# An encoder layer in one kernel: wider maxima, transposed spreads, split weights kept in DRAM, and attention exponentials handled two key tiles at a time

## The chip, the cores and the metric

The kernel runs as one program on one core of a Trainium2 chip (trn2). The metric is device time in microseconds for one execution; lower is better. Before the change three timed runs gave 3049.92, 3058.68 and 3075.47 us, with a median of 3058.68 us. One further execution was taken with the hardware profiler; all rows shown here come from it.

In the rows PE is the matrix engine, PEld its loading of the stationary operand, DVE the vector engine, ACT the scalar engine, POOL the third elementwise engine, and SP the engine whose queue issues nearly all the DMAs. L149 is line 149 of the kernel file. Every engine works through its own list of instructions strictly in the order in which it was written out; between engines there are only semaphores.

## What is computed

One layer of an encoder on a sequence of 2048 tokens of width 1024, all in float32. Cut to what matters:

```python
h = x @ w_in                                    # 2048 x 1024 -> q, k, v of A; low-rank q, kv of B; u, v of C
y_a = dilated attention, 6 heads of 64, patterns (128,1), (512,4), (2048,16), ALiBi,
      each a band of 64 keys to either side at its dilation, merged by log-sum-exp
c_q = rms(h[...]) * q_norm;  q = c_q @ w_q_up   # 6 heads, 64 plain + 32 rotary columns
c_kv = rms(h[...]) * kv_norm; kv = c_kv @ w_kv_up
y_b = softmax(q_full @ k_full.T * 96**-0.5) @ v # 6 heads, all 2048 keys
y_c = u * (w_s @ layer_norm(v) + b_s)           # in chunks of 128 tokens, 4 groups
y = concat(rms(y_a), rms(y_b), rms(y_c)) * mix_norm
x = layer_norm(ALPHA * x + y @ w_out)
f = square(relu(x @ w_ff1 + b_ff1)) @ w_ff2 + b_ff2
out = layer_norm(ALPHA * x + f)
```

The result has to agree with float32. The kernel gets there by splitting every operand into a rounded part (`h`, "high") and the rest (`l`, "low"), both in a reduced float32 type, and adding three matrix products: high by high, low by high and high by low. `mm3` (lines 148 to 151) is that triple; most of PE's time is spent in it.

## The kernel before

The program runs through five stages, whose borders can be read from the trace.

**First columns (about 0 to 225 us).** `latent_columns` takes the sequence in four blocks of 512 tokens. `load_x` fetches the eight 128-row pieces of x for a block, and ACT and DVE split each into high and low. Weights are fetched by `load_wf`, split likewise and kept. PE computes the low-rank columns (`psf`), the gating columns (`psg`) and, one block behind, the projections up to the heads' q, k and v (`psk`, `psq`, `psv`). Results go to scratch tensors in DRAM.

**Projection with latent attention (about 225 to 690 us), then dilated attention with latent attention (to about 1450 us), then the output projection with the rest of latent attention (to about 1700 us).** The function `mixers` interleaves two streams: latent attention (`latent`) always, and one filler after the other (`projection`, `dilated`, `out_projection`). Fixed rates (RATE_P, RATE_D, RATE_O) say how many filler steps follow a latent step; the Tile framework then places the instructions by its own estimate of when their operands are ready, and the result is one fixed list for each engine.

*Projection* fetches x again for blocks 0 to 2 (the last block's x is still there), splits it again, and for each block fetches the 768 columns of weights for q and k of A in twelve pieces and those of v in four (`load_w`, line 454), splitting each piece on ACT (L460) and DVE (L461). So every weight is split four times. Results are again stored in high and low parts in DRAM.

*Latent attention* works on 24 steps (6 heads by 4 blocks of 512 queries) of 16 key tiles each. For one key tile of 128 keys: three products give the scores `st` (L612 to L614); ACT takes the exponential twice, once in float32 (`pr`, L619) and once rounded (`ph`, L620); POOL subtracts them to the low part `pl` (L622); DVE adds `pr` to the running sum `ac` (L637; for key tile 8 POOL does it); and PE multiplies the values by `ph` and by `pl` into `av` (L644, L645). The maxima that are subtracted are found one or two steps ahead: 16 products `mx` (L593), each with a reduction on DVE (L594), and a last reduction `m4` whose four columns PE turns into a row (`mr`, L601). At the end of a step PE sums `ac` over the partitions with four products by a column of ones (`dn`, L665), DVE takes the reciprocal, and `spread` (L164) multiplies that column, repeated 64 times, by the identity, which puts it along the free axis of 64 partitions (`rb`). `spread` is also used with 128 partitions in the first stage and in the output projection.

*Dilated attention* has 20 groups of tiles in each of 6 heads. A first pass finds maxima: for each tile one product `amx` of 64 rows (queries by keys, high parts only, L866) and one fused DVE operation (L871). A second pass makes the scores with two products of 128 and 65 rows (L939, L940), the exponential, and the product with the values (L996). In SBUF the tile `QA` holds the high part of q twice (rows 0 to 63 and 64 to 127), and `KA` holds the high part of k above its low part.

**Feed-forward (about 1700 us to the end).** Two large products with a Strassen-like scheme of seven products each; nothing in it is touched.

## Time and profile before

| what | value |
|---|---|
| median of three runs | 3058.68 us (3049.92 to 3075.47) |
| the profiled execution's own time | 3056.2 us |
| its span, first to last instruction | 3054.4 us |
| PE busy | 2900.1 us, 95% of the span |
| PE weight loads busy | 2311.9 us, 76% |
| DVE busy | 2154.3 us, 71% |
| POOL busy | 1653.3 us, 54% |
| ACT busy | 1336.7 us, 44% |
| mean granted clock of PE | 0.962 of full |
| moved by DMA | 314.02 MB, mean 103 GB/s |

How to read it: busy time is the time in which an instruction of the engine was under way. Matrix products are pipelined, so one that is listed with 0.39 us may be followed by the next 0.23 us after its start; the distance between two starts is what a product costs PE. A busy PE is therefore not a PE at its peak. The granted clock is 1.00 when PE runs at 2.4 GHz and 0.50 when it runs at 1.2 GHz; other values are means over a stretch that has both.

### The profile page before, as it was taken

The page shows a single profiled execution, that of the slowest core. Times are in us where ns is not written, and L with a number is a line of the kernel's source. Part 1 is how long each engine was busy: PE and PEld are TensorE (multiplying, and loading weights), DVE is VectorE, ACT ScalarE, POOL GpSimd, SP SyncE. Part 2 cuts the span into 40 slices and gives each one's busy share as a digit, 9 for nine tenths or more (in the row PEclk, how much of TensorE's full clock was granted, in tenths as well). Part 3 has the DMA queues.
Part 4 walks back from the last instruction along what each step waited for, and adds up shares of the span by engine and source line. Part 5 has one row for each costly group of instructions (what it writes and reads, how often), then busy time and mean ns, then how long its engine had stood idle before and what let it go on. Part 6 is the DMA issues. An engine that isn't in the chain of part 4 may idle for free. (4 is left out here: it accounts for less than half of the span.)

```text
span 3054.4 us, 38546 instructions
## 1 busy us (share of the span) xinstructions
PE 2900.1 (95%) x12716; PEld 2311.9 (76%) x12716; DVE 2154.3 (71%) x3519; ACT 1336.7 (44%) x2504; POOL 1653.3 (54%) x1251
## 2 busy tenths in 40 slices
PE   9999899999999999998899999989999999999996
PEld 7776777887776777777787778867887877777774
DVE  4247889878877878788776843383335787778899
ACT  4325455556543544455554534353434322223333
POOL 1015556557644544456865454454445765656667
PEclk9999999999998999898999999999999999999998
DMA  5345334236022342213255533333334422222222
GB/s 165 125 136 162 107 106 128 79 116 128 14 59 47 76 88 48 54 41 89 90 174 181 162 122 111 108 115 119 106 108 166 138 80 83 83 77 76 83 66 97
DMA packets 267762, 314.02 MB, mean 103 GB/s; under 512 B 91805, under 2 KB 157981, under 8 KB 267037
## 3 DMA queue, kind: packets, MB, share of 16 engines
q1 hardware_dynamic: 254248, 295.82, 32.5%
q10 hardware_dynamic: 13312, 15.73, 1.4%
q8 instruction: 100, 1.64, 0.2%
q14 instruction: 102, 0.83, 0.1%
HBM read 209.72 MB, written 98.60 MB: 101 GB/s over the span
## 5 line engine op out<-in xcount | busy, mean ns | idle before, releaser
L622 POOL TENSOR_TENSOR pl<-pr,ph 128x512 fp32r<-128x512 f32 x384 | 553.3, 1453 | 410.8 <-ACT ph L620 271.8
L637 DVE TENSOR_TENSOR ac<-ac,pr 128x512 f32<-128x512 f32 x312 | 355.1, 1138 | 65.1 <-ACT pr L619 56.3
L1572 DVE TENSOR_TENSOR acc<-o,acc 128x512 f32<-128x512 f32 x416 | 275.2, 682 | 112.0 <-PE o L151 109.5
L619 ACT ACTIVATE pr<-st 128x512 f32<-128x512 f32 x384 | 227.9, 597 | 252.6 <-PE st L614 228.5
L594 DVE TENSOR_REDUCE m<-mx 128x1 f32<-128x512 f32 x384 | 254.9, 681 | 56.9 <-PE mx L593 56.0
L620 ACT ACTIVATE ph<-st 128x512 fp32r<-128x512 f32 x384 | 224.4, 596 | 43.9 <-PE av L644 39.2
L644 PE MATMUL av<-ph,VV 128*128 128x512 f32 x384 | 163.8, 426 | 14.1 <-DVE y L659 13.8
L645 PE MATMUL av<-pl,VV 128*128 128x512 f32 x384 | 167.9, 437 | 7.9 <-POOL pl L622 7.9
L612 PE MATMUL st<-QH,KL 96*128 96x512 f32 x384 | 167.6, 436 | 4.8 <-ACT ph L620 3.5
L593 PE MATMUL mx<-KH,QH 96*128 96x512 f32 x384 | 158.8, 435 | 12.2 <-DVE UV L424 4.6
L613 PE MATMUL st<-QL,KH 96*128 96x512 f32 x384 | 158.8, 414 | 0.0
L614 PE MATMUL st<-QH,KH 97*128 97x512 f32 x384 | 158.4, 415 | 0.0
L996 PE MATMUL aav<-apr,v 128*65 128x128 f32 (+3 forms) x624 | 123.8, 344 | 4.2 <-ACT apr L965 4.0
L1500 DVE TENSOR_TENSOR t<-t,h 128x512 f32<-128x512 f32 x32 | 21.9, 686 | 138.3 <-PE h L151 127.0
L871 DVE CUSTOM_DVE_ANT_0 jk<-amx,bias 128x256 bf16<-128x256 f32 (+2 forms) x288 | 103.2, 358 | 17.1 <-PE amx L866 9.9
L996 PEld LDWEIGHTS aav<-apr,v 128*65 128x65 f32 x624 | 85.6, 149 | 38.6 <-issue 9.3
L965 ACT ACTIVATE apr<-tt 128x192 f32<-128x192 f32 (+2 forms) x180 | 78.4, 467 | 82.9 <-PE aav L996 53.6
L939 PE MATMUL ast<-QA,KA 128*128 128x256 f32 (+1 forms) x288 | 105.7, 372 | 0.2 <-ACT ph L620 0.2
L149 PE MATMUL po<-woh,y 128*128 128x512 f32 x256 | 104.2, 407 | 0.0
L940 PE MATMUL ast<-QB,KB 65*128 65x256 f32 (+1 forms) x288 | 102.2, 368 | 1.5 <-DMA QB<-amr 1.0
L644 PEld LDWEIGHTS av<-ph,VV 128*128 128x128 f32 x384 | 79.1, 206 | 30.7 <-DVE y L659 16.9
L150 PE MATMUL po<-woh,y 128*128 128x512 f32 x256 | 101.5, 396 | 0.0
(9014 smaller groups left out, 8775.8 us busy)
## 6 DMA issues: line engine op xcount, KB each, us to landing
A<-in_w SPq DMA_DIRECT2D x128, 256.0 KB, 2.7
hid_d<-t SPq DMA_DIRECT2D x128, 256.0 KB, 3.0
A<-hid_d SPq DMA_DIRECT2D x128, 256.0 KB, 2.9
B<-in_w_ff SPq DMA_DIRECT2D x64, 256.0 KB, 4.2
xr<-in_xT SPq DMA_DIRECT2D x56, 256.0 KB, 3.3
wr<-in_wf SPq DMA_DIRECT2D x48, 256.0 KB, 3.3
yr<-y_d SPq DMA_DIRECT2D x64, 128.0 KB, 2.7
xt<-in_x SPq DMA_DIRECT2D x32, 256.0 KB, 3.4
```

Of the source, the lines that this page charges most:

```text
L593: pe.matmul(ps, s["QH"][0:96, qt * P:(qt + 1) * P], kh[0:96, kc * TB:(kc + 1) * TB], start=True, stop=True)
L594: dve.tensor_reduce(s["m16"][:, qt, kc:kc + 1], ps, AX.X, ALU.max)
L612: pe.matmul(st, kl[0:96, kk], s["QH"][0:96], start=True, stop=False)
L613: pe.matmul(st, kh[0:96, kk], s["QL"][0:96], start=False, stop=False)
L619: act.activation(pr, st, AF.Exp, scale=SC)
L620: act.activation(ph, st, AF.Exp, scale=SC)
L622: pool.tensor_tensor(pl, pr, f(ph), op=ALU.subtract)
L637: (pool if kt in AC_POOL else dve).tensor_tensor(s["ac"], s["pr"] if kt == 1 else s["ac"], pr, op=ALU.add)
L644: pe.matmul(s["av"], VV[h][:, kt], ph, start=(kt == 0), stop=False)
L645: pe.matmul(s["av"], VV[h][:, kt], pl, start=False, stop=(kt == NT - 1))
L996: pe.matmul(s[key][0:65, c0:c0 + w], s["V"][p][:, units[u][2] + j], pr[:, a0:a0 + w], start=(first[key] == i), stop=(last[key] == i), skip ...
L1572: dve.tensor_tensor(t, ps, t, op=ALU.add)
```

## The change

There are four parts, and sizes of tile pools are cut to make room.

1. *Maxima of dilated attention.* The 64-row products of the first pass become 128-row products: `QA` and `KA` are used whole, so the product is high q by the sum of high and low k.
2. *Spreads.* `spread` uses the transposing form of the product for the repeated column, always on 128 partitions. The row `mr` of the latent maxima is made by `spread` as well.
3. *Split parts kept in DRAM.* In the first stage x's high and low parts are stored for blocks 0 to 2 (`xs_d`), and the weights of the projection are fetched and split once, in nine pieces of 128 x 1024, and stored (`ws_d`). The projection then fetches the parts, and splits nothing.
4. *Two key tiles at a time.* `pr`, `ph` and `pl` become tiles of two key tiles. ACT still works on one key tile at a time; POOL subtracts and DVE adds once for two, on 128 x 1024. The running sum has two halves, so the sum over partitions takes eight products in place of four. All additions are on DVE.

The pools: `pr`, `ph` and `pl` have 2 buffers of a pair (before 4, 3 and 3 of a single tile); the three value tiles of dilated attention share one tag with 2 buffers; `rb`, `yr`, `sq` lose one buffer each.

```diff
-RB = 3
-ME = 3
+RB = 2
+ME = 2
-MP = 4
-AC_POOL = (8,)
+MP = 2
+ACB = 2
...
+    xs_d = [[dt_([P, KD, TB], f"xs_d{b}{x}") for x in "hl"] for b in range(NB - 1)]
+    ws_d = [[dt_([P, 1024], f"ws_d{i}{x}") for x in "hl"] for i in range(9)]
...
-    def spread(ps, cols, rows):
+    def spread(ps, cols):
         for j in range(cols.shape[-1]):
-            pe.matmul(ps[0:rows, j * P:(j + 1) * P], cols[:, j:j + 1].to_broadcast([P, rows]), ident, start=True, stop=True)
+            pe.transpose(ps[:, j * P:(j + 1) * P], cols[:, j:j + 1].to_broadcast([P, P]), ident)
...
+            def split_dilated(i):
+                src = a["wf"][3 + i] if i < 6 else a["wv"][:, (i - 6) * 1024:(i - 5) * 1024]
+                for x, t in zip(range(2), load_wf(wp, f"d{i}", src, "wd", 1)):
+                    dma(ws_d[i][x], t)
...
                 xs = load_x(xp, b, dve, X_BUFS, wp, XR, first if b == 0 else ())
+                if b < NB - 1:
+                    for k in range(KD):
+                        for x in range(2):
+                            dma(xs_d[b][x][:, k], xs[k][x])
...
+                    if b and 4 * (b - 1) + t < 9:
+                        split_dilated(4 * (b - 1) + t)
...
             def load_w(nm, src):
-                w = src.shape[-1]
-                wr = wp.tile([P, 768], F32, tag="wr", name=f"wr{nm}")
-                dma(wr[:, :w], src)
                 h = wp.tile([P, 768], F32R, tag="wh", name=f"wh{nm}", bufs=4)
                 l = wp.tile([P, 768], F32R, tag="wl", name=f"wl{nm}", bufs=4)
-                with hp("PW"):
-                    act.copy(h[:, :w], wr[:, :w])
-                    dve.tensor_tensor(l[:, :w], wr[:, :w], f(h[:, :w]), op=ALU.subtract)
+                for t, d in zip((h, l), src):
+                    for lo, part in d:
+                        dma(t[:, lo:lo + part.shape[-1]], part)
                 return h, l
...
-                    xs = load_x(xp, b, dve, X_BUFS, wp, 3)
+                    xs = []
+                    for k in range(KD):
+                        xs.append(tuple(xp.tile([P, TB], F32R, tag=f"x{x}", name=f"x{x}p{b}_{k}", bufs=X_BUFS) for x in "hl"))
+                        for x in range(2):
+                            dma(xs[k][x], xs_d[b][x][:, k])
...
-                    for j in range(4):
-                        pe.transpose(mr[0:1, j * P:(j + 1) * P], m4[:, j:j + 1], ident)
+                    spread(mr, m4)
                     with hp("LQ"):
-                        act.copy(s["QH"][96:97, :], mr[0:1])
+                        act.copy(s["QH"][96:97, :], mr[96:97])
...
+            if kt % 2 == 0:
+                s["pp"] = (ep.tile([P, 2, TB], F32, tag="pr", name=f"pr{nm}", bufs=MP),
+                           ep.tile([P, 2, TB], F32R, tag="ph", name=f"ph{nm}"), ep.tile([P, 2, TB], F32R, tag="pl", name=f"pl{nm}"))
+            pr, ph, pl = s["pp"]
+            i = kt % 2
             with hp("LE"):
-                act.activation(pr, st, AF.Exp, scale=SC)
-                act.activation(ph, st, AF.Exp, scale=SC)
-            with hp("LP"):
-                pool.tensor_tensor(pl, pr, f(ph), op=ALU.subtract)
-                sums.append((s, kt, pr))
-            if len(sums) > ALAG:
-                add_up(*sums.pop(0))
+                act.activation(pr[:, i], st, AF.Exp, scale=SC)
+                act.activation(ph[:, i], st, AF.Exp, scale=SC)
+            if i:
+                with hp("LP"):
+                    pool.tensor_tensor(pl, pr, f(ph), op=ALU.subtract)
+                add_up(s, kt // 2, pr)
...
-                (pool if kt in AC_POOL else dve).tensor_tensor(s["ac"], s["pr"] if kt == 1 else s["ac"], pr, op=ALU.add)
+                dve.tensor_tensor(s["ac"], s["pr"] if i == 1 else s["ac"], pr, op=ALU.add)
...
-                    pe.matmul(dn[:, j:j + 1], s["ac"][:, j * P:(j + 1) * P], ones[:, 0:1], start=True, stop=True)
+                    for i in range(2):
+                        pe.matmul(dn[:, j:j + 1], s["ac"][:, i, j * P:(j + 1) * P], ones[:, 0:1], start=i == 0, stop=i == 1)
...
-                v = qp.tile([P, d, NT // d, 66], F32, tag=f"v{p}", name=f"v{h}_{p}", bufs=1)
+                v = qp.tile([P, NT, 66], F32, tag="v", name=f"v{h}_{p}").rearrange("p (r n) c -> p r n c", r=d)
...
-                        pe.matmul(bank_cols(ps, p, tl, j), tok(s["QA"][0:64], d, r, n * P, P),
-                                  cols(s["KA"][0:64], p, tl, j), start=True, stop=True, skip_group_check=True)
+                        pe.matmul(bank_cols(ps, p, tl, j), tok(s["QA"], d, r, n * P, P),
+                                  cols(s["KA"], p, tl, j), start=True, stop=True, skip_group_check=True)
```

How the lists of three places read before and now follows; each row is the kernel's line, the operation, what it writes and reads, and the size.

The queue of SP at the start of the program, before: `xr` is a raw piece of x for block 0, the three `wfrc` are the raw weights of the first, second and third output tile (the last two 128 x 1024).

```order
L143 DMA wfrc_185<-in_wf 128x512
L143 DMA xr_2_209<-in_xT 128x512
L143 DMA xr_3_215<-in_xT 128x512
L143 DMA wfrc_245<-in_wf 128x1024
L143 DMA xr_4_221<-in_xT 128x512
L143 DMA gains<-in_cgain 128x3
L143 DMA tbc_702<-in_cs 128x512
L143 DMA xr_5_227<-in_xT 128x512
L143 DMA wfrc_251<-in_wf 128x1024
```

The same queue now, from the 15th row on; `xs_d0h` and `xs_d0l` are the stores of block 0's parts.

```order
L144 DMA xs_d0h<-xh_2_235 128x512
L144 DMA xr_6_257<-in_xT 128x512
L144 DMA xr_7_263<-in_xT 128x512
L144 DMA xs_d0l<-xl_2_236 128x512
L144 DMA xs_d0h<-xh_3_241 128x512
L144 DMA xs_d0l<-xl_3_242 128x512
L144 DMA xs_d0h<-xh_4_247 128x512
L144 DMA xs_d0l<-xl_4_248 128x512
L144 DMA xs_d0h<-xh_5_253 128x512
L144 DMA wfrc_285<-in_wf 128x1024
L144 DMA xs_d0l<-xl_5_254 128x512
L144 DMA wfrc_291<-in_wf 128x1024
```

The weights of the second output tile stood eighth in the queue, with four pieces of x ahead of them; now they stand behind all eight pieces of x and eleven stores.

PE in latent attention, head 2, second block of queries, before: `st` are scores of a key tile (last number but one), `av` the products with the values.

```order
L612 MATMUL st_1_9_7103<-QH_1_5922,KL_1896 128x512
L613 MATMUL st_1_9_7103<-QL_1_5923,KH_1895 128x512
L614 MATMUL st_1_9_7103<-QH_1_5922,KH_1895 128x512
L645 MATMUL av_1_6963<-pl_1_5_6992,VV_4832 128x512
L644 MATMUL av_1_6963<-ph_1_6_7007,VV_4832 128x512
L612 MATMUL st_1_10_7119<-QH_1_5922,KL_1896 128x512
L613 MATMUL st_1_10_7119<-QL_1_5923,KH_1895 128x512
L614 MATMUL st_1_10_7119<-QH_1_5922,KH_1895 128x512
L645 MATMUL av_1_6963<-pl_1_6_7008,VV_4832 128x512
L644 MATMUL av_1_6963<-ph_1_7_7044,VV_4832 128x512
```

The same place now; `pl_1_4` holds key tiles 4 and 5.

```order
L638 MATMUL st_1_10_6754<-QH_1_5665,KL_2040 128x512
L639 MATMUL st_1_10_6754<-QL_1_5666,KH_2039 128x512
L640 MATMUL st_1_10_6754<-QH_1_5665,KH_2039 128x512
L671 MATMUL av_1_6607<-pl_1_4_6599,VV_4696 128x512
L670 MATMUL av_1_6607<-ph_1_4_6598,VV_4696 128x512
L671 MATMUL av_1_6607<-pl_1_4_6599,VV_4696 128x512
L670 MATMUL av_1_6607<-ph_1_6_6652,VV_4696 128x512
L620 MATMUL mx_3_2_6642<-KH_2039,QH_3_6486 128x512
L620 MATMUL mx_3_3_6656<-KH_2039,QH_3_6486 128x512
L671 MATMUL av_1_6607<-pl_1_6_6653,VV_4696 128x512
L670 MATMUL av_1_6607<-ph_1_6_6652,VV_4696 128x512
```

Scores ran four key tiles ahead of the product with `pl` at this place; now they are five to six ahead, and products with the values come in runs of four.

The queue of SP in the projection, where block 0 follows on block 3, before: `xr` and `wr` are raw pieces, `va_d` a store of v.

```order
L143 DMA va_d<-va_0_2701 128x384
L143 DMA va_d<-va_1_2814 128x384
L143 DMA va_d<-va_2_2947 128x384
L143 DMA xr_4_3092<-in_xT 128x512
L143 DMA wr_10_3248<-in_wf 128x512
L143 DMA xr_5_3098<-in_xT 128x512
L143 DMA y_d_0_114<-y_0_2880 64x512
L143 DMA xr_6_3104<-in_xT 128x512
```

The same place now; `xhp`, `xlp`, `wh` and `wl` are the parts that the products read.

```order
L144 DMA xhp_5_3143<-xs_d0h 128x512
L144 DMA xlp_5_3144<-xs_d0l 128x512
L144 DMA xhp_6_3147<-xs_d0h 128x512
L144 DMA xlp_6_3148<-xs_d0l 128x512
L144 DMA xhp_7_3151<-xs_d0h 128x512
L144 DMA y_d_0_138<-y_0_2946 64x512
L144 DMA va_d<-va_3_3120 128x384
L144 DMA xlp_7_3152<-xs_d0l 128x512
L144 DMA wh_00_3155<-ws_d0h 128x512
L144 DMA wl_00_3156<-ws_d0l 128x512
```

A raw piece went into a buffer of its own; a part goes straight into the buffer that PE's products of the block before read, so its DMA waits for them, and the next block's first weights are now behind them in the queue.

## Rows read from the trace of the kernel before

**Rows 1.** The page, busy time by engine: share of the span, number of instructions

```profile
PE 2900.1 (95%) x12716; PEld 2311.9 (76%) x12716; DVE 2154.3 (71%) x3519; ACT 1336.7 (44%) x2504; POOL 1653.3 (54%) x1251
```

**Rows 2.** Stages: busy us (instructions) of PE, PEld, DVE, ACT, POOL; PEclk, DMA share, GB/s

```profile
0.00:225.00 225.00, 216.90 (x965) 172.35 (x966) 84.88 (x140) 73.62 (x119) 27.17 (x30) 0.99 0.43 140
225.00:690.00 465.00, 433.63 (x1946) 350.63 (x1946) 386.75 (x541) 248.93 (x460) 264.71 (x184) 0.96 0.37 117
690.00:1450.00 760.00, 726.60 (x3230) 565.80 (x3228) 609.09 (x1307) 381.38 (x763) 414.63 (x317) 0.92 0.31 65
```

**Rows 3.** PE in order of time, dilated attention: start us, duration us, line, operands, rows*columns, count

```profile
1229.16 0.29 PE L939 MATMUL ast<-QA,KA 128*128 128x256 f32 x1
1229.28 0.28 PE L940 MATMUL ast<-QB,KB 65*128 65x256 f32 x1
1229.40 0.40 PE L644 MATMUL av<-ph,VV 128*128 128x512 f32 x1
1229.73 0.50 PE L866 MATMUL amx<-KA,QA 64*128 64x256 f32 x2
1230.16 0.50 PE L612 MATMUL st<-QH,KL 96*128 96x512 f32 x1
1230.50 0.39 PE L613 MATMUL st<-QL,KH 96*128 96x512 f32 x1
1230.73 0.39 PE L614 MATMUL st<-QH,KH 97*128 97x512 f32 x1
```

**Rows 4.** PE in order of time, a run of four maxima of the third pattern

```profile
1191.62 1.12 PE L866 MATMUL amx<-KA,QA 64*128 64x256 f32 x4
1192.68 0.54 PE L996 MATMUL aav<-apr,v 128*65 128x192 f32 x2
```

**Rows 5.** PE in order of time, a spread over 64 partitions in the projection

```profile
417.91 0.39 PE L150 MATMUL psp<-xh,wl 128*128 128x512 f32 x1
418.23 1.09 PE L164 MATMUL rb<-ident,rc 128*64 128x128 f32 x8
419.24 0.50 PE L151 MATMUL psp<-xl,wh 128*128 128x512 f32 x1
419.58 0.39 PE L149 MATMUL psp<-xh,wh 128*128 128x512 f32 x1
```

**Rows 6.** PE in order of time, four transposes in the output projection

```profile
1498.03 0.66 PE L1250 MATMUL pt<-ident,xt 128*128 128x128 f32 x4 [0.86 <-DVE xt L1152]
1498.44 0.48 PE L149 MATMUL po<-woh,y 128*128 128x512 f32 x1
1498.76 0.40 PE L150 MATMUL po<-woh,y 128*128 128x512 f32 x1
```

**Rows 7.** PE in order of time, the sum over partitions of one step

```profile
454.62 0.95 PE L665 MATMUL dn<-ones,ac 128*128 128x1 f32 x8
455.43 0.48 PE L612 MATMUL st<-QH,KL 96*128 96x512 f32 x1
```

**Rows 8.** Single lines: ns min/median/max; first and last start us; forms

```profile
L637 DVE TENSOR_TENSOR ac<-ac,pr x312: 669/840/4866, 280.9 to 1557.8; 128x512 f32<-128x512 f32 x156
L191 DVE TENSOR_TENSOR wclg<-wfrg,wchg x4: 1206/1218/1225, 20.7 to 31.1; 128x1024 fp32r<-128x1024 f32 x4
```

**Rows 9.** The page, costliest groups: busy us, mean ns; idle before, and its releaser

```profile
L622 POOL TENSOR_TENSOR pl<-pr,ph 128x512 fp32r<-128x512 f32 x384 | 553.3, 1453 | 410.8 <-ACT ph L620 271.8
L637 DVE TENSOR_TENSOR ac<-ac,pr 128x512 f32<-128x512 f32 x312 | 355.1, 1138 | 65.1 <-ACT pr L619 56.3
```

**Rows 10.** Waits of PE from 225 to 1450 us: total us, times, longest us

```profile
PE mr L601 <- DVE m L598: 12.5, 8, 5.6
...
PE av L645 <- POOL pl L622: 7.4, 4, 2.7
```

**Rows 11.** Two stretches, columns as in rows 2

```profile
6.00:24.00 18.00, 16.98 (x61) 12.57 (x61) 10.29 (x14) 10.13 (x14) 0.00 (x0) 1.00 0.96 335
950.00:990.00 40.00, 39.10 (x132) 28.62 (x131) 24.97 (x70) 12.63 (x28) 11.88 (x10) 0.74 0.13 22
```

More of the change, by code (lines that the diff above doesn't have):

```diff
@@ L58 @@
 D_MRATE = 2.2
-MP = 4
-AC_POOL = (8,)
+MP = 2
+ACB = 2
 ON_POOL = "qks"
-ALAG = 0
 HP_L = 0
@@ L239, in norm @@
                     rb = acc_bank(f"rb{b}{g}")
-                    spread(rb, rr[b][:, g], P)
+                    spread(rb, rr[b][:, g])
                     for i in tiles:
@@ L499, in projection @@
                     yield
-                w = [load_w(f"{b}v{i}", a["wv"][:, i * 768:(i + 1) * 768]) for i in range(4)]
+                w = [load_w(f"{b}v{i}", split_w(6, i * 768, 768)) for i in range(4)]
                 for t in range(4):
@@ L646, in value @@
             if kt == NT - 1:
-                while sums and sums[0][0] is s:
-                    add_up(*sums.pop(0))
                 finish(s)
@@ L669, in store @@
                 rb = bank("mx", f"rb{nm}")
-                spread(rb, rc, 64)
+                spread(rb, rc)
                 dve.tensor_tensor(y, y, rb[0:64], op=ALU.mult)
@@ L1219, in raws @@
             rstd(sm, r, ss[:, 0:4], 4, 1.0 / 384, "orst")
-            rb = page(yp, "rb", f"orb{ob}", 2)
+            rb = page(yp, "rb", f"orb{ob}", 1)
             pb = bank("mx", f"opb{ob}")
-            spread(pb, r, P)
+            spread(pb, r)
             act.copy(rb, pb)
```

31 lines of the change are left out of this document (19 added, 12 removed).

## The prediction

> **What bounds the kernel now.** I read the busy times first, then the stages, then single products on PE, and the waits last. PE is busy for 2900.1 of 3054.4 us [rows 1], and in the two stages that the change touches most, 225 to 690 and 690 to 1450 us, for 434 of 465 and 727 of 760 us; DVE, the next, reaches 387 and 609 [rows 2]. The reader is to see that PE has the longest list in each of them and that its idle time there is only 31 and 33 us. But busy is not the same as well used: in the dilated stage the granted clock is 0.92 on the mean, and 0.74 in a stretch in which PE never stops for long [rows 2, 11]. So three things can shorten these 1225 us: products that cost PE less, the idle 64 us, and the clock. Work taken from DVE, ACT or POOL counts only through the last two. PE's list for the feed-forward does not change.
>
> All sums below are against the profiled execution: span 3054.4 us, its own time 3056.2 us, which is 2.5 us under the median 3058.7 us. So I add 4.3 us to a span to compare with the median.
>
> **Wider maxima: -35 us.** Two products of 256 columns with 128 rows start 0.12 us apart (1229.16, 1229.28, 1229.40). The pair `amx` with 64 rows takes 0.43 us (1229.73 to 1230.16), the product ahead of it 0.33 and the one behind it 0.34 us, where the one after that takes 0.23 [rows 3]. So PE pays about 0.10 us on the way into a run of 64-row products, 0.11 us on the way out, and 0.19 us inside. PE's list has 101 such runs. In and out: 101 x 0.21 = 21 us. Inside: the first pattern reads whole columns, 8 pairs in 6 heads, 48 x 0.19 = 9 us. The second and third patterns read every fourth or sixteenth column and may be slow for that reason alone: a run of four takes 1.06 us [rows 4], 0.27 us each; I put 5 us on them, between nothing and 24 runs x 0.58 = 14 us (at 0.12 each). Together 35 us, bounds 21 and 44. The Trainium skill speaks against this: "TensorE: Matmul & The Clock Gate" (Back-to-back issue gap and Why this matters for your kernels) has a product cost its columns, and a 32-row product the time of a 128-row one. By that rule this part is worth nothing and the sum is 35 us higher; rows 3 disagree for a 64-row run among 128-row ones, and I go by them.
>
> **Spreads: -24 us.** A spread over 64 partitions is recorded as eight products. They take 1.01 us (418.23 to 419.24), the product ahead 0.32 and the one behind 0.34 us against 0.23: 1.21 us in all [rows 5]. Four transposes take 0.41 us, the product behind them 0.32: 0.50 us [rows 6]. 24 steps x 0.71 = 17 us. The 64 spreads over 128 partitions lose one record in two, 64 x 0.11 = 7 us. The row `mr` keeps its four transposes and only gets wider: nothing. Bounds 14 and 28 us.
>
> **Sum over partitions: +21 us.** Eight records take 0.81 us, the first of them short, so 0.11 us each [rows 7]. Eight more in 24 steps: 24 x 8 x 0.11 = 21 us. These stand in PE's list among other products, nothing hides them.
>
> **Splits moved: +10 us at the start, no cost after it.** Before, the weights of the second output tile are the eighth DMA; now eleven stores of 262 kB and four more pieces of x stand ahead of them. From 6 to 24 us the DMA is at 0.96 of its time and 335 GB/s [rows 11], so the 2.9 MB of stores alone are 8.6 us. PE has only the 24 products of the first tile to do meanwhile, and waits: I take 7 us, bounds 0 and 15. The rest of the first stage gets 27 MB on top of 31 MB; 58 MB in 225 us is 258 GB/s, under the 335 seen, so it is mostly hidden; I put 3 us on it, up to 30. In the projection the DMAs of weights and x double, from 25 to 50 MB in 465 us, 54 GB/s on top of 117: hidden. The 88 subtractions taken from DVE cost between 0.67 and 1.14 us each [rows 8, 9], 59 to 100 us of 387; nine of 1.22 us come in the first stage, where DVE is busy for 85 of 225 us.
>
> **Pairs of key tiles: no cost on PE, relief on DVE.** An addition alone on 512 columns takes 0.67 us at the least and 1.14 on the mean; a DVE operation on 1024 columns with two inputs from SBUF takes 1.22 us while POOL is nearly idle [rows 8, 9, 2]. So 336 additions of 1.14 us (383 us) become 168 of 1.22 to 2.28 us; I take 1.9, as DVE will still wait for POOL, 319 us, a relief of 64 us in 1280. POOL's 384 subtractions of 1.45 us become 192; between 1.45 (no longer than now) and 2.9 us each, I take 2.6. POOL is busy for 265 of 465 and 415 of 760 us, so there is room. The products with the values come later: they stand five to six key tiles behind the scores where it was four.
>
> **Idle time and clock: -38 us.** PE's waits for DVE and POOL from 225 to 1450 us are many and short; the longest row is 12.5 us, for the last reduction of the maxima, which stands behind other work on DVE [rows 10]. With 140 us less on DVE I give back 20 of the 64 idle us, bounds +10 and -45. The clock: 0.92 over 760 us means 122 us at 1.2 GHz, in which PE does 61 us of work at full speed. No row says why it falls; in 950 to 990 us it is 0.74 while PE is busy for 39.1 of 40 us, with short products and 64-row runs among the others, so gaps alone are not it [rows 11]. I give back 18 of the 61 us, bounds 0 and -50.
>
> **Sum:** -35 - 24 + 21 + 10 - 20 - 18 = -66 us. 3054.4 - 66 = 2988 us of span, 2992 us beside the median. Own range 2965 to 3018 us. Chance 0.44.
>
> **Rivals.** *Only PE's list shrinks.* The static lists are made with estimates, and DVE still waits for POOL's longer turns, so neither idle time nor clock improve: -28 us, 3031 us (3018 to 3045). For it: the waits of rows 10 are spread over many causes. Chance 0.18.
>
> *More is given back.* The slow clock in the dilated stage goes with the 64-row runs, and DVE's relief halves the idle time: -28 - 50 - 32 = -110 us, 2949 us. For it: the low clock there comes without long gaps. Chance 0.16.
>
> *The first stage is bound by DMA.* Stores delay x for the next block, and the stage costs 40 us in place of 10: 3022 us. For it: the start is already at 0.96 of the DMA's time. Against: after it only 0.43 [rows 2]. Chance 0.07.
>
> *64 rows cost nothing by themselves.* The change does not do what I read into it, and the skill's rule holds: 3027 us. Chance 0.05.
>
> *Slower: PE waits for the pairs.* The low part of a pair is ready only after two key tiles and one subtraction of POOL that is up to 1.45 us longer, and only two pairs have buffers; PE's list is fixed, so a late `pl` stops everything behind it. If half of the 192 pairs hold PE for 1.45 us: 139 us, 3131 us; it outweighs the gain of 66 us from 46 pairs on. Against: PE waits for `pl` only 7.4 us now [rows 10], and a pair has about 6.7 us (1280 us for 192) for 2.6 on POOL. Chance 0.07.
>
> *Transposes let the clock fall.* The Trainium skill ("TensorE: Matmul & The Clock Gate", Part 4) says that transposes don't count as activity for the clock gate. If the clock of both middle stages fell by another 0.04 for that reason, 1225 us x 0.04 = 49 us, 3041 us. Against it: nothing in rows 6, where transposes stand among products and these go on at 0.23 to 0.32 us. Chance 0.03.
>
> **How the numbers follow.** A difference under 1% (31 us) cannot be told from none here. Faster, under 3028 us: the first case, the third, and shares of those that end near 3028 (0.05 of the list alone, 0.05 of DMA, 0.03 of 64 rows): 0.73. Within 1%, up to 3089 us: 0.20. Slower: 0.07. The range from 2935 to 3045 us leaves out the pairs and the far ends of the others.
>
> **What would show it.** Right: `amx` pairs about 0.24 to 0.45 us with 0.23 us ahead and behind; a spread near 0.45 us; the records of `dn` doubled; the first gating product some 7 us later; additions near 1.9 us; the clock from 690 to 1450 us near 0.94. Wrong: PE's waits for `pl` over 50 us, a first stage over 240 us, or a dilated stage not shorter than 720 us.

## The result, and the profile after

The changed kernel takes 3017.48 us in the median of 6 runs (3014.22 to 3024.24), the kernel before 3063.93 us in the runs beside it (6 runs). The ratio is 0.9856, with a 95% interval from 0.9823 to 0.9888: 46 us, or 1.4%, faster. The forecast was 2992 us. The profiled execution has a span of 3014.7 us, 39.7 us under that of before where 66 were forecast; its own time is 3016.5 us.

Busy time by engine on the page after, which answers to [rows 1]:

```profile
PE 2847.0 (94%) x12748; PEld 2315.2 (77%) x12748; DVE 2042.0 (68%) x3272; ACT 1289.8 (43%) x2425; POOL 1606.6 (53%) x1035
```

The three stretches of [rows 2], same columns, after:

```profile
0.00:225.00 225.00, 209.84 (x906) 163.44 (x907) 88.29 (x131) 77.33 (x121) 22.99 (x25) 0.98 0.69 244
225.00:690.00 465.00, 443.24 (x2040) 366.17 (x2039) 288.22 (x418) 206.12 (x387) 243.96 (x120) 0.96 0.56 179
690.00:1450.00 760.00, 707.51 (x3387) 592.11 (x3386) 608.88 (x1236) 400.28 (x804) 431.11 (x207) 0.93 0.32 68
```

PE has lost 53 us of busy time and DVE 112. But in the third stretch PE now stands idle for 52 us, where it was 33, and the clock is 0.93, hardly above 0.92. In the second DVE fell from 387 to 288 us and PE's idle time from 31 to 22: this is where DVE's relief can be seen. In the third DVE is busy for 609 us in both kernels.

The single steps, in PE's order of time after. A pair of maxima of the first pattern (it answers to [rows 3]), a spread in the projection ([rows 5]) and the sum over partitions ([rows 7]):

```profile
1118.68 0.39 PE L640 MATMUL st<-QH,KH 97*128 97x512 f32 x1
1118.91 0.40 PE L891 MATMUL amx<-KA,QA 128*128 128x256 f32 x2
1119.15 0.40 PE L671 MATMUL av<-pl,VV 128*128 128x512 f32 x1
...
410.07 0.40 PE L152 MATMUL psp<-xlp,wh 128*128 128x512 f32 x1
410.31 0.60 PE L165 MATMUL rb<-ident,rc 128*128 128x128 f32 x4
410.66 0.48 PE L150 MATMUL psp<-xhp,wh 128*128 128x512 f32 x1
410.99 0.40 PE L638 MATMUL st<-QH,KL 96*128 96x512 f32 x1
...
1100.91 1.84 PE L690 MATMUL dn<-ones,ac 128*128 128x1 f32 x16
```

The start of `amx` is 0.23 us behind that of the product ahead of it, and the pair takes 0.24 us in place of 0.43: no way in, no way out, nothing inside. The spread costs 0.35 us and 0.10 more on the product behind it, 0.45 us in all. The 16 records of `dn` take 0.115 us each.

DVE's additions and POOL's subtractions in pairs, on the page's list of groups ([rows 9]), and the additions as single lines ([rows 8]):

```profile
L652 POOL TENSOR_TENSOR pl<-pr,ph 128x1024 fp32r<-128x1024 f32 x192 | 522.5, 2724 | 397.2 <-ACT ph L649 258.6
...
L663 DVE TENSOR_TENSOR ac<-ac,pr 128x1024 f32<-128x1024 f32 x144 | 275.2, 1911 | 51.2 <-ACT pr L648 50.6
```

```profile
L663 DVE TENSOR_TENSOR ac<-ac,pr x144: 1189/1226/6565, 301.6 to 1522.9; 128x1024 f32<-128x1024 f32 x144
```

1.91 and 2.72 us, against 1.9 and 2.6 in the forecast. PE's waits from 225 to 1450 us, as in [rows 10]:

```profile
PE av L671 <- POOL pl L652: 12.2, 11, 2.7
PE ast L964 <- ACT ph L649: 9.7, 3, 8.5
PE amx L891 <- DVE m L621: 5.8, 4, 3.7
...
PE mr L165 <- DVE m L625: 1.2, 3, 0.8
```

The wait for the last reduction of the maxima went from 12.5 to 1.2 us. The one for the pairs, the slower rival, is 12.2 us: it didn't come.

Where did the time go? I cut the span at the same four places of PE's order in every kernel: the start of the third product of the first latent score (L614 before, L640 now), the last product of the projection, the last product of the dilated values, the last of the output projection. In us:

| kernel | start | projection | dilated | output projection | feed-forward |
|---|---|---|---|---|---|
| before | 275.9 | 447.6 | 681.5 | 306.9 | 1342.5 |
| after | 289.3 | 425.9 | 649.2 | 308.3 | 1342.1 |

The first stage lost 13 us, the projection won 22 and the dilated stage 32. The second cut is by cause. The distance from each product's start to the next one's is split: its columns at 2.4 GHz (0.23 us for 512, and 0.12 us at the least), what they take longer where the granted clock was at 1.2, what is left if that is under 0.35 us (short gaps), and if it is more (idle). The border between columns and short gaps is uncertain by some 6 us, their sum by 1; I call the sum PE's list. Sums over the first four stages, in us:

| | columns | low clock | short gaps | idle |
|---|---|---|---|---|
| before | 1360.5 | 67.2 | 184.6 | 94.7 |
| after | 1365.0 | 59.4 | 133.7 | 110.4 |
| difference | +4.5 | -7.8 | -50.9 | +15.7 |

PE's list became 46 us shorter, where the forecast's three terms on it made 38. Idle time and clock gave back nothing: together +8, where the forecast had them at -28 with the start's 10 in it.

### The profile page after: what moved, and what is told of

It is laid out like the page before. It is cut to its first block, busy times and chain, and to the rows that moved or that the text cites. A ratio compares the mean times of both kernels' runs of the same rounds, so it can differ in the third digit from the quotient of the medians.

```text
span 3014.7 us, 37857 instructions
## 1 busy us (share of the span) xinstructions
PE 2847.0 (94%) x12748; PEld 2315.2 (77%) x12748; DVE 2042.0 (68%) x3272; ACT 1289.8 (43%) x2425; POOL 1606.6 (53%) x1035
## 5 line engine op out<-in xcount | busy, mean ns | idle before, releaser
L652 POOL TENSOR_TENSOR pl<-pr,ph 128x1024 fp32r<-128x1024 f32 x192 | 522.5, 2724 | 397.2 <-ACT ph L649 258.6
L663 DVE TENSOR_TENSOR ac<-ac,pr 128x1024 f32<-128x1024 f32 x144 | 275.2, 1911 | 51.2 <-ACT pr L648 50.6
L671 PE MATMUL av<-pl,VV 128*128 128x512 f32 x384 | 160.4, 418 | 13.0 <-POOL pl L652 13.0
L670 PE MATMUL av<-ph,VV 128*128 128x512 f32 x384 | 157.5, 410 | 3.0 <-DVE y L683 3.0
L640 PE MATMUL st<-QH,KH 97*128 97x512 f32 x384 | 158.0, 413 | 0.0
L1021 PE MATMUL aav<-apr,v 128*65 128x128 f32 (+3 forms) x624 | 115.3, 328 | 3.3 <-DVE mc L896 1.9
L150 PE MATMUL po<-woh,y 128*128 128x512 f32 x256 | 104.2, 408 | 0.0
L620 PEld LDWEIGHTS mx<-KH,QH 96*128 96x128 f32 x384 | 74.9, 201 | 36.5 <-DVE m L621 10.3
```

Source lines behind the costliest of these rows:

```text
L150: pe.matmul(ps, wh, xh, start=first, stop=False, skip_group_check=reopen)
L620: pe.matmul(ps, s["QH"][0:96, qt * P:(qt + 1) * P], kh[0:96, kc * TB:(kc + 1) * TB], start=True, stop=True)
L652: pool.tensor_tensor(pl, pr, f(ph), op=ALU.subtract)
L663: dve.tensor_tensor(s["ac"], s["pr"] if i == 1 else s["ac"], pr, op=ALU.add)
L1021: pe.matmul(s[key][0:65, c0:c0 + w], s["V"][p][:, units[u][2] + j], pr[:, a0:a0 + w], start=(first[key] == i), stop=(last[key] == i), skip ...
```

## Experiments

All times are medians of their runs, ratios are against the kernel before, run beside them on the same chip. The change and the experiments ran in five sets, in which the kernel before had medians of 3057.3 to 3063.9 us: a difference of a few microseconds between runs of different sets is not told from none. Sums by cause come from one profiled execution each, and the part of the low clock in them changes from one execution to the next; the granted clock of the whole execution is known for every run, and is given where an argument rests on the clock.

### Taking back one part at a time

The maxima back on 64 rows (run max64):

```diff
-pe.matmul(bank_cols(ps, p, tl, j), tok(s["QA"], d, r, n * P, P),
-          cols(s["KA"], p, tl, j), start=True, ...
+pe.matmul(bank_cols(ps, p, tl, j), tok(s["QA"][0:64], d, r, n * P, P),
+          cols(s["KA"][0:64], p, tl, j), start=True, ...
```

> The changed kernel with the dilated maxima back on 64 rows; all else as in the change. Theory (a product with 64 rows among 128-row ones costs PE time on the way in and out): from the rows of both traces at the high clock, a pair goes from 0.24 + 0.45 + 0.24 us back to 0.33 + 0.51 + 0.34, 0.25 us more, and a run of four from 0.24 + 0.83 + 0.25 to 0.33 + 1.05 + 0.34, 0.41 us more; 60 pairs and 34 runs of four make 29 us, bounds 20 and 40 with the clock: 3046 us against 3017. Rival (rows cost nothing, the gain came from other parts): 3017 us within 5. Rival (the clock falls with the 64-row runs): more than 45 us slower, with the low clock in the dilated stage back at 100 us from 61.

Measured: 3064.26 us, ratio 1.0021 (1.0002 to 1.0040). It is 47 us slower than the change and no faster than the kernel before: without this part, the rest of the change is worth nothing. Its size is that of the last rival, over 45 us, and the low clock came with it (the table under 65 rows; the granted clock of the whole execution is 0.952 to 0.958 in its twelve runs, 0.961 to 0.967 in the six of the change); but the way in and out of the first theory is there as well. The same kind of place on PE, with 64 rows:

```profile
1029.48 0.39 PE L640 MATMUL st<-QH,KH 97*128 97x512 f32 x1
1029.80 0.50 PE L891 MATMUL amx<-KA,QA 64*128 64x256 f32 x2
1030.23 0.50 PE L671 MATMUL av<-pl,VV 128*128 128x512 f32 x1
```

0.32 us ahead of the pair and 0.43 in it, as in [rows 3].

The spreads as products, and the row of the maxima one partition wide (run spread_old):

```diff
-    pe.transpose(ps[:, j * P:(j + 1) * P], cols[:, j:j + 1].to_broadcast([P, P]), ident)
+    pe.matmul(ps[0:rows, j * P:(j + 1) * P], cols[:, j:j + 1].to_broadcast([P, rows]), ident, start=True, stop=True)
...
-spread(rb, rc)
+spread(rb, rc, 64)
...
-spread(mr, m4)
+for j in range(4):
+    pe.transpose(mr[0:1, j * P:(j + 1) * P], m4[:, j:j + 1], ident)
```

> The changed kernel with all spreads as products with the identity again (64 columns of output partitions in the latent stage, 128 elsewhere), and the row of the maxima as four transposes one partition wide; all else as in the change. Theory: 24 steps x 0.77 us (1.21 against 0.44) = 18 us, and 64 spreads x 0.11 us = 7 us: 25 us slower, 3042 us. Rival (transposes let the clock fall, so that a part of their gain is lost): less than 12 us slower, with less time at the low clock than in the changed kernel. Rival (spreads stand off the path, PE waits there anyway): within 5 us of 3017.

Measured: 3030.7 us, 0.9917 (0.9888 to 0.9947): 13 us slower than the change, half of what was expected. Over the first four stages PE's list is 34 us longer than in the change, idle time 10 us shorter and the cost of the low clock 5 us lower. The projection took 14.5 us longer, the dilated stage only 1: there columns and short gaps grew by 14 us and idle time shrank by 12. So in the dilated stage PE waits for others in the time that it saves. The rival with the clock stays open, at a small size: the granted clock of the whole execution is 0.967 to 0.972 in these six runs and 0.961 to 0.967 in the six of the change, 0.004 apart on the mean, which over 3015 us is 13 us at the most. But late_half_pool, below, has the same transposes and 0.971 to 0.974. The Trainium skill says that a transpose does not count as work of PE for the clock gate in the way that a product does ("TensorE: Matmul & The Clock Gate", Part 4); the two kernels' clocks point that way, and no run here shows that the transposes are the cause.

Single key tiles again (run single_tiles: four `pr`, three `ph` and `pl`, four products in `dn`, the ninth addition on POOL):

```diff
-if kt % 2 == 0:
-    s["pp"] = (ep.tile([P, 2, TB], F32, tag="pr", bufs=MP), ...)
...
-if i:
-    pool.tensor_tensor(pl, pr, f(ph), op=ALU.subtract)
-    add_up(s, kt // 2, pr)
+pool.tensor_tensor(pl, pr, f(ph), op=ALU.subtract)
+sums.append((s, kt, pr))
+add_up(*sums.pop(0))
```

> The changed kernel with the exponentials subtracted and summed one key tile at a time again (three ph and pl, four pr, the addition of the ninth tile on POOL, four records of dn a step); maxima, spreads and moved splits as in the change. Theory (the relief on DVE buys nothing, and the doubled records of dn cost 21 us): 3017 - 21 = 2996 us, and the idle time of PE in the dilated stage, which grew by 22 us with the change, goes back as well: down to 2975 us. Rival (the relief of DVE pays for the records): 3017 us within 8. Rival (the relief is what shortened the stages): slower, 3030 us and more.

Measured: 3019.53 us, 0.9871 (0.9848 to 0.9895), the change within its interval. The first rival holds: going over to pairs (DVE's busy time over the first four stages falls from 1206 to 1151 us) pays for the doubled records, and no more.

The first two parts alone, single tiles and the splits back in the projection as well (run parts_1_2):

```diff
-    if b and 4 * (b - 1) + t < 9:
-        split_dilated(4 * (b - 1) + t)
...
-    for lo, part in d:
-        dma(t[:, lo:lo + part.shape[-1]], part)
+    act.copy(h[:, :w], wr[:, :w])
+    dve.tensor_tensor(l[:, :w], wr[:, :w], f(h[:, :w]), op=ALU.subtract)
```

> The kernel before with the wider maxima and the transposed spreads alone: splits in the projection and single key tiles as before. Theory (PE's list only): 3064 - 29 - 25 = 3010 us; beside single_tiles it tells the part of the moved splits: they cost 13 us at the start and gave 22 us in the projection, so this one should be 9 us slower than single_tiles. Rival (the moved splits gain nothing in the projection, what shortened it are the spreads and the pairs): this one is 10 us faster than single_tiles.

Measured: 3014.77 us, 0.9858 (0.9833 to 0.9883). **The first two parts alone give what the whole change gives.** It is 5 us under single_tiles, between the two theories and nearer to the rival, and within the intervals no difference. The stages of the two profiled executions show where: the moved splits cost 16.1 us at the start (289.4 against 273.3) and gave 6.5 in the projection (430.1 against 436.6). In the dilated stage, in which they change no instruction, single_tiles is 9.7 us shorter, 7 of them in the cost of the low clock; over all their runs the two kernels have the same granted clock (0.966 to 0.971 and 0.966 to 0.970), so this is not shown to be the splits' doing. DVE's busy time in the projection falls with the moved splits alone. Here are its stretches in before (ending at 723 us), in this kernel (710) and in single_tiles (720), in this order:

```profile
276.00:723.00 447.00, 420.75 (x1940) 347.31 (x1940) 378.93 (x520) 242.41 (x447) 263.89 (x182) 0.96 0.32 100
```

```profile
273.00:710.00 437.00, 412.65 (x1913) 342.78 (x1912) 382.70 (x520) 243.13 (x448) 266.72 (x183) 0.97 0.33 102
```

```profile
289.00:720.00 431.00, 412.70 (x1915) 347.74 (x1915) 315.99 (x445) 202.75 (x375) 255.90 (x186) 0.96 0.50 159
```

From the second of the three to the third DVE gives up 67 us, and PE gets 6.

### 65 rows

One row more than before the change (run max65):

```diff
-tok(s["QA"], d, r, n * P, P), cols(s["KA"], p, tl, j)
+tok(s["QA"][0:65], d, r, n * P, P), cols(s["KA"][0:65], p, tl, j)
```

> The changed kernel with the dilated maxima on 65 rows, one more than before the change (the 65th row adds a piece of the low part). Theory (64 rows make PE change its way of working, and 65 do not): as the change, 3017 us within 6, with 0.24 us ahead of a pair and behind it and about 60 us at the low clock in the dilated stage. Rival (the cost and the clock go by how many rows are at work, 65 of 128): as with 64 rows, 3064 us, with more than 100 us at the low clock. Rival (two effects: the way in and out is a matter of 64, the clock of the rows): about 3040 us, with 0.24 us beside the pairs and more than 100 us at the low clock.

Measured: 3029.21 us, 0.9906 (0.9887 to 0.9925), between the two. A pair on PE:

```profile
1024.80 0.40 PE L640 MATMUL st<-QH,KH 97*128 97x512 f32 x1
1025.04 0.41 PE L891 MATMUL amx<-KA,QA 65*128 65x256 f32 x2
1025.28 0.40 PE L671 MATMUL av<-pl,VV 128*128 128x512 f32 x1
```

One row more than 64, and the way in and out is gone, 0.24 us as with 128. So it is no matter of rows at work, but of a product that fits 64. The Trainium skill has a rule for this ("TensorEngine Tiling (Array Packing)", Tiling Modes, Key Properties): products of up to 64 rows can run in another tiling mode, and a change of mode drains TensorE. The rows agree with it, with some 0.1 us on either side; that a mode is what changes can't be seen in a row. That a product costs its columns alone, as I weighed in the prediction, fails here for a product of 64 rows among longer ones.

The other 12 us are in the clock: its granted clock is 0.959 to 0.963 in six runs, against 0.961 to 0.967. The dilated stage of the change, of 64 rows and of 65, in this order:

```profile
715.00:1364.00 649.00, 607.42 (x2966) 510.61 (x2965) 517.88 (x1145) 337.02 (x680) 342.09 (x163) 0.95 0.31 64
```

```profile
712.00:1405.00 693.00, 666.06 (x2973) 523.34 (x2971) 514.46 (x1146) 339.36 (x682) 338.28 (x163) 0.90 0.29 59
```

```profile
722.00:1383.00 661.00, 621.99 (x2963) 521.17 (x2962) 517.50 (x1144) 337.02 (x679) 340.89 (x163) 0.92 0.31 62
```

In the cut by cause, for this stage alone (the last column leaves out low clock during idle time; the runs from half_records on come below):

| kernel | columns | low clock | short gaps | idle | time at 1.2 GHz |
|---|---|---|---|---|---|
| before | 467.7 | 39.0 | 146.0 | 28.8 | 101 |
| after | 475.5 | 24.6 | 98.2 | 51.0 | 61 |
| max64 | 472.9 | 47.0 | 139.8 | 32.7 | 124 |
| max65 | 472.5 | 41.1 | 100.8 | 47.2 | 97 |
| spread_old | 481.3 | 23.2 | 106.7 | 38.9 | 56 |
| single_tiles | 466.1 | 20.5 | 102.2 | 47.1 | 50 |
| half_records | 462.7 | 30.6 | 104.2 | 64.0 | 79 |
| wide_scores | 477.0 | 20.4 | 98.5 | 60.1 | 48 |
| late_half_pool | 464.8 | 18.7 | 100.6 | 59.0 | 45 |

From 64 to 128 rows: short gaps -42 (with the columns -39), low clock -22, idle +18. From 65 to 128 the short gaps stay within 3 us and the low clock gives 16. The idle time grows whenever the short gaps go.

### Wider scores

Is it the rows, then, that hold the clock? Run wide_scores:

```diff
-KB = fp.tile([65, S], F32R, name="KB")
+KB = fp.tile([P, S], F32R, name="KB")
+pool.memset(f(KB[64:128]), 0.0)
...
+dma(QB[65:128, cs_], qa_d[hp][1][o:o + 63, cs_])
...
-pe.matmul(st, kh[0:97, kk], s["QH"][0:97], start=False, stop=True)
+pe.matmul(st, kh[:, kk], s["QH"], start=False, stop=True)
```

> The changed kernel with more rows in the scores and nothing else: the second product of the dilated scores reads 128 rows in place of 65 (rows of zeros in the weights against finite rows of q), and two of the three products of the latent scores 128 in place of 96 and 97 (zeros in the weights against further copies of the maxima). The result of each product is the same. It adds 12 transfers of 258 kB and a few memsets. Theory (the clock goes by how many rows are at work, as the run with 65 rows in the maxima suggests): PE's time at the low clock between 290 and 1673 us falls from 126 us to 90 or less, which returns 14 us or more of the 52 that it costs: 3003 us or less. Rival (rows of zeros don't count, or the low clock in the run with 65 rows came from elsewhere): 3017 us within 6.

Measured: 3027.76 us, 0.9879 (0.9858 to 0.9900). The theory fails in time: 10 us slower than the change where 14 were to be won (7 us by the ratios, whose intervals overlap). The time at the low clock from 290 us to the end of the output projection is 107 us against 126, about half of the fall that was expected, but the dilated stage has 9 us more idle time and the output projection takes 4 us more. Whether rows that carry data hold the clock, and rows of zeros don't, or whether the low clock with 65 rows has another cause, stays open.

### The start

The stores of the first block's split x behind the weights (run late_stores):

```diff
-if b < NB - 1:
+def keep():
     for k in range(KD):
         for x in range(2):
             dma(xs_d[b][x][:, k], xs[k][x])
+if 0 < b < NB - 1:
+    keep()
...
 wg.append(load_wf(wp, f"g{i}", ...))
+keep()
```

> The changed kernel with the 16 stores of the first block's split x issued after the weights of the second and third output tile and of the gating, not ahead of them. Theory (the stores ahead of those weights are what delays the first stage): the 72nd product of the first tiles starts at 27 us in place of 37 and the stage ends 10 us earlier: 3007 us. Rival (the bytes cost the time, wherever they stand): 3017 us, the delay comes later in the stage.

Measured: 3008.29 us, 0.9833 (0.9817 to 0.9850): 9 us of the 10 expected. The 72nd product, the last of the first block's three tiles of 24, starts at 27.3 us in place of 37.2. PE's waits in the first 45 us of the change, and of this kernel:

```profile
PE psf L150 <- ACT xh L177: 8.4, 4, 4.7
PE psf L150 <- ACT wchc L191: 5.3, 1, 5.3
PE psf L151 <- DVE wclc L192: 0.5, 1, 0.5
```

```profile
PE psf L150 <- ACT xh L177: 6.4, 3, 4.7
```

The wait for the second tile's weights (`wchc`) is gone. The stretch of [rows 11] from 6 to 24 us, in the change and in this kernel:

```profile
6.00:24.00 18.00, 9.04 (x23) 4.90 (x22) 6.87 (x10) 6.58 (x10) 0.00 (x0) 0.95 0.98 348
```

```profile
6.00:24.00 18.00, 16.32 (x55) 12.16 (x55) 8.91 (x11) 8.01 (x11) 0.00 (x0) 1.00 1.03 358
```

The DMA is as full in both, and moves as much; only what stands first in the queue differs. PE does 16.3 us of work in place of 9.0.

### The doubled records

The halves of the sum added first, on DVE (run half_records):

```diff
+dve.tensor_tensor(s["ac"][:, 0], s["ac"][:, 0], s["ac"][:, 1], op=ALU.add)
 act.copy(y, s["av"][64:128])
...
 for j in range(4):
-    for i in range(2):
-        pe.matmul(dn[:, j:j + 1], s["ac"][:, i, j * P:(j + 1) * P], ones[:, 0:1], start=i == 0, stop=i == 1)
+    pe.matmul(dn[:, j:j + 1], s["ac"][:, 0, j * P:(j + 1) * P], ones[:, 0:1], start=True, stop=True)
```

> The changed kernel with the two halves of the pair's sum added on DVE first (one more addition of 512 columns a step), so that dn has four records a step again, not eight (each taken twice in the trace: eight and sixteen). Theory (the records stand in PE's list and nothing hides them): 24 x 8 x 0.11 = 21 us less, 2996 us. Rival (in the dilated stage PE waits for DVE, which has 24 more additions of 0.67 to 1.9 us): less than 8 us gained.

Measured: 3019.36 us, 0.9875 (0.9853 to 0.9897): nothing gained, the rival in its size. PE's list became 18 us shorter over the first four stages, near the forecast, but idle time grew by 20, by 13 of them in the dilated stage. PE's longest row of waits from 225 to 1450 us:

```profile
PE mr L165 <- DVE m L625: 11.3, 6, 3.5
```

It was 1.2 us in the change. The longest of these six waits, 3.5 us, stands behind one of the 24 additions on DVE, which took 3.25 us:

```profile
782.22 3.25 DVE L682 TENSOR_TENSOR ac<-ac 128x512 f32<-128x512 f32 x1
785.39 0.16 DVE L625 TENSOR_REDUCE m<-m 128x4 f32<-128x16 f32 x1
```

Ahead of the reductions of the other five stand additions of pairs (three times), other reductions of the maxima and a split of weights. So on this row the new additions themselves account for 3.5 us; where the rest of the 20 comes from was not followed up.

Both edits together (run late_and_half):

> Both together: the stores behind the weights, and the halves added on DVE. Theory: the two gains add, 3017 - 10 - 21 = 2986 us. Rival (either is taken by a wait elsewhere): over 3000 us.

Measured: 3001.53 us, 0.9813 (0.9797 to 0.9830): 7 us under late_stores. That is the rival (over 3000 us), if only just.

The same addition on POOL, behind the step's last subtraction, and the stores late (run late_half_pool):

```diff
+pool.tensor_tensor(s["ac"][:, 0], s["ac"][:, 0], s["ac"][:, 1], op=ALU.add)
 rc = fp.tile([P, 4], F32, tag="rc", name=f"rc{nm}")
```

> The stores behind the weights, and the halves of the sum added on POOL, not on DVE, after the last subtraction of a step. Theory (with the halves on DVE it was the 24 additions ahead of the maxima's last reduction that held PE, 10.5 us on the row of the maxima alone; POOL is busy for half of the stage): 3008 us of late_stores less the 21 us of records: 2987 us. Rival (the records stand where PE waits for DVE anyway): 3000 us or more, as with the halves on DVE.

Measured: **2991.18 us, 0.9764 (0.9743 to 0.9785)**, 17 us under late_stores where 21 were expected, and 26 under the change: the fastest version of all that ran. In its trace the wait is 5.2 us, and POOL's additions are short:

```profile
PE mr L165 <- DVE m L628: 5.2, 4, 1.8
```

```profile
L687 POOL TENSOR_TENSOR ac<-ac x24: 1268/1286/1647, 320.3 to 1496.3; 128x512 f32<-128x512 f32 x24
```

The time is near the theory's, its reason is not shown. Up to the end of the output projection, late_and_half (halves on DVE) and late_half_pool (on POOL), in this order:

```profile
0.00:1659.00 1659.00, 1549.47 (x7162) 1274.03 (x7163) 1193.00 (x2085) 788.86 (x1553) 822.72 (x471) 0.96 0.46 136
```

```profile
0.00:1644.00 1644.00, 1534.17 (x7163) 1262.81 (x7164) 1163.20 (x2061) 787.50 (x1554) 854.91 (x495) 0.97 0.47 137
```

PE stands idle for 109.5 us in the one and 109.8 in the other, and for 91 in late_stores: the shorter list brought some 18 us of idle time with either engine. What is less on POOL is PE's busy time, and by the cut by cause 12 of these 15 us are the low clock: the granted clock of the whole execution is 0.969 to 0.970 in the four runs of late_and_half, 0.966 to 0.969 in the four of late_stores and 0.971 to 0.974 in the five of late_half_pool. Why the clock is higher stays open.

With the wider scores on top (run late_half_wide):

> The stores behind the weights, the halves on POOL and the wider scores together. Theory (the gains add): 14 us under late_half_pool, some 2973 us. Rival (wider scores give nothing): as late_half_pool within 6 us.

Measured: 2993.42 us, 0.9770 (0.9748 to 0.9792). The rival: they give nothing.

### What the pairs are worth

The stores late, single tiles as in single_tiles (run late_single):

> The stores behind the weights, with single key tiles as in single_tiles: against late_half_pool (2991 us) it tells what the pairs are worth once the doubled records are gone. Theory (the pairs' relief of DVE and POOL gives PE 15 to 20 us, which the doubled records took away in the change): 3019.5 - 9 = 3010 us, some 19 us over late_half_pool. Rival (the pairs give nothing; late_half_pool gains by the records alone, which single tiles don't have either): 2991 us within 6.

Measured: 3009.83 us, 0.9840 (0.9808 to 0.9871), 19 us over late_half_pool, as the theory had it. So the pairs are worth time once the doubled records are gone; but it does not come as the theory says, by fewer waits of PE in the stages with attention. Up to the end of the output projection PE's idle time is that of late_half_pool, 108.6 us:

```profile
0.00:1658.00 1658.00, 1549.36 (x7163) 1266.22 (x7164) 1209.18 (x2226) 792.19 (x1553) 875.88 (x687) 0.96 0.47 135
```

Of the 14 us between the two up to there, 6 are PE's list and 9 the low clock (0.963 to 0.972 over the six runs). Another 8 us come behind it, where PE in late_single waits for DVE's last tiles of the output projection, and not in late_half_pool:

```profile
PE pt L1280 <- DVE xt L1182: 10.0, 2, 6.9
```

The same row is 7.3 us in single_tiles and 10.0 in parts_1_2.

## Why the prediction was right, and where it was not

**Wider maxima, -35 us (21 to 44).** Right in mechanism, and too small: taking them back costs 47 us. In the dilated stage PE's list is 39 us of it, between the forecast and its upper bound. To that comes what the low clock gave (22) less what new idle time took (18), both of which I had priced elsewhere and not tied to this part: 43 us there, in one profile each. That all patterns lose their way in and out, and the strided ones keep what is inside, was right: on the median at the high clock a run of four went from 1.05 to 0.83 us.

**Spreads, -24 us.** The step's 0.45 us came as forecast. PE's list is 34 us shorter for them, more than forecast, and 13 us reached the end: idle time took 10, and the low clock may have taken 5.

**Sum over partitions, +21 us.** Right as a length of PE's list: 20 us of columns left with the halves on POOL or on DVE. "Nothing hides them" was wrong: without them idle time grew by 17 to 20 us (half_records against the change, late_and_half and late_half_pool against late_stores). That late_half_pool still won 17 us came from the clock.

**Splits, +10 us at the start.** Right in mechanism, 13 us in size: 10.9 us were there at the 72nd product, where the forecast had 7, and the clock fell (0.95 in the stretch above, where it was 1.00 in [rows 11]). The rest of the first stage cost next to nothing, as forecast. The projection's transfers were hidden too.

**Pairs: no cost on PE, 64 us of relief.** 1.91 and 2.72 us for 1.9 and 2.6; 55 us of relief over the four stages (single_tiles against the change). What it gave PE by fewer waits shows at the end of the output projection alone (late_single). The rival with 46 late pairs had its sign in the trace: 12.2 us.

**Idle time, -20 us: the step that failed.** "With 140 us less on DVE I give back 20 of the 64 idle us" took DVE's busy sum for what PE waits for. In the projection, where DVE lost 101 us, it was so (idle 28.7 to 11.6 us). In the dilated stage, where DVE lost 26, idle time grew from 28.8 to 51.0 us, and 18 of these 22 came with the wider maxima alone (max64 against the change). The reason is argued, not shown: as PE's list becomes shorter, late instructions that it had covered are covered no more. For it speaks that idle time grew with every edit that made the list more than 10 us shorter. The two longest waits of the changed kernel show what such an instruction looks like. First ACT and PE around 856 us, then DVE, POOL and PE from 1103 us:

```profile
855.55 0.62 ACT L568 CAST KH<-kr 64x512 fp32r<-64x512 f32 x1 [9.29 <-DMA kr<-kn_d]
...
857.34 0.60 PE L964 MATMUL ast<-QA,KA 128*128 128x256 f32 x1 [8.47 <-ACT ph L649]
```

```profile
1102.73 1.26 POOL L569 TENSOR_TENSOR KL<-kr,KH 64x512 fp32r<-64x512 f32 x1 [8.07 <-ACT KH L568]
...
1103.18 5.44 DVE L663 TENSOR_TENSOR ac<-ac,pr 128x1024 f32<-128x1024 f32 x1 [4.75 <-ACT pr L648]
...
1103.95 2.35 POOL L652 TENSOR_TENSOR pl<-pr,ph 128x1024 fp32r<-128x1024 f32 x1
...
1106.27 1.26 POOL L592 TENSOR_TENSOR VV<-vraw,VV 128x512 fp32r<-128x512 f32 x1
...
1107.51 2.23 POOL L569 TENSOR_TENSOR KL<-kr,KH 64x512 fp32r<-64x512 f32 x1
...
1109.38 0.58 PE L891 MATMUL amx<-KA,QA 128*128 128x256 f32 x1 [3.66 <-DVE m L621]
```

In the first, ACT stands for 9.3 us at the load of the next head's keys, its exponentials wait behind that, and PE 8.5 us for a bank of scores; in the kernel before, ACT's wait at the same load was 4.4 us and PE's 2.7:

```profile
865.49 0.62 ACT L541 CAST KH<-kr 64x512 fp32r<-64x512 f32 x1 [4.42 <-DMA kr<-kn_d]
```

```profile
866.26 0.50 PE L593 MATMUL mx<-KH,QH 96*128 96x512 f32 x1 [2.74 <-ACT acc L975]
```

In the second, one addition of a pair takes 5.44 us, where its minimum is 1.19: POOL's operations follow each other without a break from 1102.73 to 1107.53, and the addition ends 1.09 us after that, while POOL's next operation takes 2.23 us where the same took 1.26 at 1102.73. The reduction that PE waits for stands behind the addition, and PE waits for 3.7 us. The Trainium skill has POOL share its way to SBUF with DVE, in contention with DVE's instructions that have two inputs from SBUF ("GPSIMD Engine Reference", Specifications); the trace agrees, with 5.44 against 1.19 us. What is faster on the mean is still a longer single hold: 6.57 us at the most, where it was 4.87 [rows 8]. In max64 the same two waits of PE are 5.1 and 3.9 us, so they make 3 of the 18 us that came with the wider maxima. The rest of the 51 us are many rows of less than 5 us, and were not tested one by one.

**Clock, -18 us.** It gave 14 us in the dilated stage and 5 in the projection (low clock 39.0 to 24.6 and 14.8 to 9.6), and lost 5 at the start and 7 in the output projection: -8 in all. From 690 to 1450 us it reached 0.93, not 0.94. In the dilated stage the gain came with the rows of the maxima (max64, max65), where the prediction named no cause.

So the likeliest case had its sign and its list right, and 3017 us lies at the upper end of its own range (2965 to 3018), within it by half a microsecond and so by luck: PE's list gave 8 us more than forecast, idle time and clock 36 us less. What happened is nearer to the rival in which only PE's list shrinks (3031 us). The rival with 64 rows that cost nothing is refuted by max64 and max65, the one with the DMA-bound first stage by its 13 us and by late_stores. In the one with the transposes the clock of both middle stages falls by 0.04; between spread_old and the change it was 0.004 over the whole execution.

## What to carry to other kernels

Look first for products that fit 64 rows among full ones: here their being made wider was worth all that the change gave, and one row more than 64 was worth three quarters of that. Busy time taken from an engine that is not the bound is worth what single late instructions it removes, and is read from the waits: 67 us of DVE gave PE 6 here. Time taken from PE's own list counts in full only while the others keep up: 18 to 22 us of records less brought 17 to 20 us of idle time, whichever engine got the additions. A new transfer cost here by what stood behind it in the queue, not by its bytes.

## What was not expected of the hardware

- The cost of a run of 64-row products among longer ones: 0.08 us in and 0.09 out with 64 rows, nothing with 65 (max64, max65, medians at the high clock: 0.32 and 0.34 us against 0.24 and 0.25).
- With 64 rows in the maxima PE works at 1.2 GHz for 101 and 124 us of the dilated stage, with 65 for 97, in the eleven kernels with 128 rows for 39 to 79 (one profile each). Over all runs the granted clock is 0.952 to 0.958 in max64, 0.959 to 0.963 in max65 and 0.961 to 0.967 in the change. The cause is open.
- DVE's addition of 1024 columns takes 1.19 us at the least and up to 6.57 beside POOL: the mean of 1.91 hides holds of over 5 us. The one at 1103.18 us ended only after three operations of POOL in a row, not between two of them.
